# Pinning the recurrence's products in TensorE's queue to the order of the program

## The chip, the cores and the metric

The kernel runs on one core of a Trainium2 chip, in one launch. The metric is the device time of one execution, in microseconds (us); lower is better. Before the change the median of three runs is 3521.82 us.

## The reference, cut to what matters

The model is two transformer-like blocks of two layers each, over 512 latent tokens and, in the first block, 256 context tokens. The change touches one mixer of the first block alone, a gated linear recurrence (mLSTM) with 4 heads of 96 features, which runs forward and backward:

```python
dmat = jnp.where(tri, b[..., :, None] - b[..., None, :] + ib[..., None, :], -jnp.inf)
w_intra = jnp.exp(dmat - m_t[..., None])
s = jnp.einsum("bhtd,bhsd->bhts", qb, kb) * w_intra
num = jnp.einsum("bhts,bhsv->bhtv", s, vb) + ...
den = s.sum(axis=-1) + ...
h = num / jnp.maximum(jnp.abs(den), jnp.exp(-m_t))[..., None]
```

The kernel computes it without the carried state, as a masked quadratic form: for each head and direction, scores of keys against queries, times an exponential of gates, times the values.

## The kernel before

Activations lie with features on the 128 partitions and tokens along the free dimension. Most of the time goes into dense products of three passes each (`mm3`, lines 144, 145 and 147), whose weights SyncE loads, and ScalarE (`whi`, L121) and GpSimd (`wlo`, L122) split in two halves.

The recurrence is `mlstm`. It runs three times: over the context in layer 0 (one block of 256 queries), and over the latents in layers 0 and 1 (two blocks Q = 0 and 1). Below, a *stage* (Q, p) is one block Q of 256 queries against one pair p of key blocks of 128; p = 2 is the context. A latent recurrence goes through (0,2), (0,0), (0,1), (1,2), (1,1), (1,0). Where p equals Q a stage is diagonal: it holds both directions with a triangular mask; p = 2 has both directions without a mask; (0,1) and (1,0) have one direction.

- `scores` has four steps in a stage, one for each head. A step computes the scores of a head, two products (L953, tile `qM` by `kM` into a bank `pm`). For each direction it takes a bank `pt` and, for each of two key blocks kk, computes the gate rows into half of that bank (L960, `rows` by `sel`), adds the mask where the stage is diagonal (L964), reads the half with ScalarE's exponential into `D` (L966), and multiplies on VectorE into `W` (L968, L970). There are two `pt` banks and three `D` buffers, shared with other work.
- `values` follows for the stage before: in each of four steps (the ones column, then three columns of the values) every direction and key block gives four products, one for each head (L983). Each fills 32 of TensorE's 128 columns, at tile positions 0, 32, 64 and 96, and adds into the bank group `p`. Four such neighbours are called a quad here.
- `weave` alternates a step of scores and a step of values of the stage before. In the first stage there is no stage before, so its steps stand alone. After the last values of a block comes `mlstm_out` (den, L1014 to L1033), with three products at L1028 that need VectorE and ScalarE first, in another `pt` bank.
- Around the recurrence other generators are woven in: the Fourier mixer (L786 to L805) beside the first stage, and the first part of the output projection, groups of 15 products at L144, L145 and L147 (tiles `y` and `whi`, `wlo`), beside the stages from (1,2) on.

The program issues the products in this order, but the framework's scheduler does not keep it: on each engine it places instructions by its own estimate of when they are ready. The `pt` half of the second key block is written only after ScalarE has read the first half of that bank: each second L960 waits for the L966 before it.

A product with both operands in full fp32 (L953, L983, L1028) leaves two records in the trace, so "x28" of L983 is 14 products; L960 and L964 leave one.

Of the kernel before, what the change touches and what calls it, by code (L numbers as in the profile page):

```python
# [67 lines left out]
def weave(a, b, na, nb):  # L68

    credit = 0.0  # L70
    for _ in a:
        credit += nb / na
        while credit >= 1:
            credit -= 1
            if next(b, None) is None:
                credit = -1e9
        yield True
    for _ in b:
        yield True
# [10 lines left out]
class Kernel:  # L90
    def __init__(self, nc, tc, st, d, at):
# [10 lines left out]
        self.dram = pool("dram", 1, space=bass.MemoryType.DRAM)  # L102
        self.n_split = self.n_project = 0


    def col(self, name, i=0, n=1, rows=slice(0, 128)):
        o, m = self.at[name]
        assert i + n <= m
        return self.cols[rows, o + i:o + i + n]
# [812 lines left out]
    def mlstm(self, s, l, o, ctx, rows_cc, ys):  # L922
        nc, d, n = self.nc, self.d, s.n
        own = ctx is None
        nk = n if own else n + 256
        rows, cc, negm = rows_cc
        o["gm"] = self.times(f"gm{l}{s.name}", self.col(f"gm{l}", 0, 3), -0.5 / 96)
        VM, qk = o["VM"], o["qk"]
        q, k = [], []
        for h in range(4):  # L930
            t = self.new("hq", [96, n], "qM")
            nc.sync.dma_start(out=t, in_=qk[96 * h:96 * h + 96])
            q.append(t)
            t = self.new("hk", [96, nk], "kM")
            nc.sync.dma_start(out=t[:, 0:n], in_=qk[384 + 96 * h:480 + 96 * h])
            if not own:
                nc.sync.dma_start(out=t[:, n:], in_=ctx["kM"][384 + 96 * h:480 + 96 * h])
            k.append(t)
        nq = n // 256
        first = [] if own else [nq]  # L940
        acc, late = {}, iter(())

        def seen(Q, p, dr, kk):

            return slice(0, 256) if p != Q or kk == dr else slice(128 * kk, 128 * kk + 128)

        def scores(Q, p, dirs, W):
            cQ = slice(256 * Q, 256 * Q + 256)
            for h in range(4):
                sp = self.psum("pm", [128, 2, 256])  # L950
                for kk in range(2):
                    c = 256 * p + 128 * kk
                    nc.tensor.matmul(sp[:, kk], k[h][:, c:c + 128], q[h][:, cQ], start=True, stop=True)  # L953
                for dr in dirs:
                    rp = self.psum("pt", [128, 2, 256])
                    D = self.new("ta", [128, 2, 256], "D")
                    w = self.new("W", [128, 2, 256], "W")
                    for kk in range(2):
                        r = 32 * dr + 6 * h + 2 * p + kk
                        nc.tensor.matmul(rp[:, kk], self.sel2[:, r:r + 1].to_broadcast([128, 128]), rows[:, cQ],  # L960
                                         start=True, stop=p != Q)
                        if p == Q:

                            nc.tensor.matmul(rp[:, kk, 128 * kk:128 * kk + 128], self.identb, self.tri[:, dr], start=False, stop=True)  # L964
                        T = seen(Q, p, dr, kk)
                        nc.scalar.activation(out=D[:, kk, T], in_=rp[:, kk, T], func=AF.Exp, bias=cc[:, 2 * p + kk, r:r + 1])  # L966
                        if p == Q:
                            nc.vector.tensor_tensor(out=w[:, kk, T], in0=sp[:, kk, T], in1=D[:, kk, T], op=ALU.mult)  # L968
                    if p != Q:
                        nc.vector.tensor_tensor(out=w, in0=sp, in1=D, op=ALU.mult)  # L970
                    W[dr, h] = w
                yield True

        def values(Q, p, dirs, W, ends):
            for j in (3, 0, 1, 2):
                for dr in dirs:
                    if (Q, dr) not in acc:
                        acc[Q, dr] = self.psum("p2", [128, 4, 256])
                    for i, kk in enumerate((dr, 1 - dr)):
                        T = seen(Q, p, dr, kk)  # L980
                        for h in range(4):
                            lhs = VM[2 * p + kk][:, 96 * h + 32 * j:96 * h + 32 * j + 32] if j < 3 else self.ones[:, 0:32]
                            nc.tensor.matmul(acc[Q, dr][32 * h:32 * h + 32, j, T], lhs, W[dr, h][:, kk, T],  # L983
                                             start=p == ends[dr][0] and i == 0 and j in (3, 0),
                                             stop=p == ends[dr][1] and i == 1 and j in (1, 2), tile_position=(0, 32 * h))
                yield True

        for Q in range(nq):
            sets = [first + list(range(0, Q + 1)), first + list(range(Q, nq))]
            order = first + [Q] + [p for p in range(nq) if p != Q]  # L990
            lists = [[p for p in order if p in x] for x in sets]
            ends = [(x[0], x[-1]) for x in lists]
            for p in order:
                dirs = [dr for dr in range(2) if p in sets[dr]]
                W = {}
                yield from weave(scores(Q, p, dirs, W), late, 4, 4 if p != order[0] or not Q else 6)
                late = values(Q, p, dirs, W, ends)
                if p == order[-1]:
                    late = self.chain(late, self.mlstm_out(s, l, o, Q, acc, negm, ys))
        yield from late  # L1000
# [689 lines left out]
```

## Time and profile before

| | |
|---|---|
| median of 3 runs | 3521.82 us (3521.39 to 3522.93) |
| the profiled execution, its own time | 3521.57 us |
| span of its instructions | 3519.8 us |
| TensorE matmul busy | 3356.4 us, 95% of the span |
| VectorE, ScalarE, GpSimd busy | 49%, 45%, 32% |
| TensorE's mean granted clock | 0.977 of 2.4 GHz |
| the recurrence in the context | 190.8 to 220.5 us |
| the recurrence in the latents, layer 0 | 380.2 to about 500 us |
| the recurrence in the latents, layer 1 | 1371.2 to about 1496 us |

TensorE's busy time contains the modelled tails of its pipelined products: a product counts as busy for longer than it keeps the next one from starting. So the start of one product to the start of the next is the better measure of what it costs, and a full share of busy time does not say that the engine does useful work at its peak.

### The profile page before, as it was taken

To read this page: it belongs to the slowest core of one execution; us is meant where nothing else is said; L and a number is where in the kernel's file an instruction comes from. 1 tells how busy PE (TensorE), PEld (TensorE's weight loads), DVE (VectorE), ACT (ScalarE), POOL (GpSimd) and SP (SyncE) were. 2 spreads that over 40 slices of the span, in tenths; PEclk is the share of its full clock that TensorE was granted. 3 is DMA by queue.
4 is the path that set the end of the run, shared out by engine and by line. 5 is a ranking of instruction groups with operands and counts; after the bars stand their busy time and mean duration, and the time that the engine had idled before them with its cause. 6 is when DMAs were issued, how large, how long until landed. Compare 5 with 4: busy or idle time off the path is not lost.

```text
span 3519.8 us, 47211 instructions
## 1 busy us (share of the span) xinstructions
PE 3356.4 (95%) x18518; PEld 2632.2 (75%) x18518; DVE 1728.1 (49%) x2728; ACT 1583.8 (45%) x2824; POOL 1139.9 (32%) x539
## 2 busy tenths in 40 slices
PE   6999998999998899989999999999999999999999
PEld 4666667888887666678878657887888757888887
DVE  5754358443336763374325865464314756453111
ACT  5545445242234554353333666543334656543333
POOL 1222024222235321144444212444444312343443
PEclk8999999999999999999999999999999999999999
DMA  7722124333334321045442101236422101222222
GB/s 266 265 89 63 43 67 142 132 117 123 114 108 155 108 75 57 21 134 196 164 144 99 67 31 53 88 106 213 164 96 90 66 31 59 76 94 90 96 96 96
DMA packets 146705, 377.87 MB, mean 107 GB/s; under 512 B 16737, under 2 KB 32690, under 8 KB 146354
## 3 DMA queue, kind: packets, MB, share of 16 engines
q1 hardware_dynamic: 146482, 374.85, 31.7%
q8 instruction: 146, 2.39, 0.3%
q14 instruction: 77, 0.63, 0.1%
HBM read 363.48 MB, written 9.86 MB: 106 GB/s over the span
## 4 chain that ended last, share of the span: by engine, by line
PE 56%; DVE 8%; ACT 2%; DMA 2%; issue 1%; POOL 0%; SPq 0%; DVEq 0%; ACTq 0%; POOLq 0%
PE pm L144 14%; PE pm L145 14%; PE pm L147 13%; DMA g<-in_w_mod 1%; DVE y L360 1%; PE p L983 1%; PE p L1182 1%; PE pt L1200 1%; PE p L1227 1%; PE pt L1208 1%; PE pm L151 1%; PE pt L1248 1%; DVE h L388 1%; PE pt L145 1%; PE pm L953 1%
## 5 line engine op out<-in xcount | busy, mean ns | idle before, releaser
L122 POOL TENSOR_TENSOR wlo<-raw,whi 128x1024 fp32r<-128x1024 f32 (+2 forms) x461 | 1089.2, 2364 | 2189.9 <-ACT whi L121 2071.7
L121 ACT CAST whi<-raw 128x1024 fp32r<-128x1024 f32 (+2 forms) x468 | 476.8, 1019 | 1079.7 <-PE pm L145 603.1
L144 PE MATMUL pm<-h,whi 128*128 128x512 f32 (+1 forms) x2312 | 851.9, 377 | 11.3 <-DVE kr L676 5.0
L145 PE MATMUL pm<-h,whi 128*128 128x512 f32 (+1 forms) x2312 | 842.1, 372 | 2.8 <-DVE h L388 2.7
L147 PE MATMUL pm<-h,wlo 128*128 128x512 f32 x1816 | 718.1, 395 | 2.3 <-POOL wlo L122 2.3
L144 PEld LDWEIGHTS pm<-h,whi 128*128 128x128 f32 x2312 | 440.5, 191 | 107.8 <-issue 20.8
L145 PEld LDWEIGHTS pm<-h,whi 128*128 128x128 f32 x2312 | 439.9, 190 | 78.9 <-issue 5.8
L144 PE MATMUL pm<-hid,whi 128*128 128x512 f32 (+1 forms) x1280 | 457.3, 367 | 2.8 <-DVE x L459 1.5
L145 PE MATMUL pm<-hid,whi 128*128 128x512 f32 (+1 forms) x1280 | 456.2, 365 | 3.7 <-DVE hid L527 3.7
L147 PEld LDWEIGHTS pm<-h,wlo 128*128 128x128 f32 x1816 | 344.3, 190 | 76.2 <-POOL wlo L122 4.0
L147 PE MATMUL pm<-hid,wlo 128*128 128x512 f32 x976 | 381.3, 391 | 3.1 <-POOL wlo L122 3.1
L527 DVE TENSOR_TENSOR hid<-relu,hid 128x512 fp32r<-128x512 f32 (+1 forms) x169 | 180.0, 1069 | 335.4 <-ACT hid L526 335.2
L273 DVE SCALAR_TENSOR_TENSOR p<-g,svec,p 128x512 f32<-128x512 f32 x280 | 211.0, 753 | 253.8 <-DMA g<-in_w_mod 250.8
L459 DVE SCALAR_TENSOR_TENSOR x<-pm,mod,x 128x512 f32<-128x512 f32 (+1 forms) x184 | 125.4, 684 | 385.1 <-PE pm L147 379.3
L144 PEld LDWEIGHTS pm<-hid,whi 128*128 128x128 f32 x1280 | 241.4, 189 | 45.7 <-issue 4.3
L145 PEld LDWEIGHTS pm<-hid,whi 128*128 128x128 f32 x1280 | 241.1, 188 | 42.8 <-DVE hid L527 5.0
L147 PEld LDWEIGHTS pm<-hid,wlo 128*128 128x128 f32 x976 | 183.9, 188 | 42.6 <-POOL wlo L122 4.4
L521 ACT ACTIVATE relu<-pm 128x512 f32<-128x512 f32 (+1 forms) x160 | 85.4, 534 | 131.6 <-PE pm L147 131.6
L966 ACT ACTIVATE D<-pt,cc 128x256 f32<-128x256 f32 (+1 forms) x176 | 75.0, 447 | 97.4 <-PE pt L960 59.5
L339 DVE TENSOR_TENSOR acc<-acc,sq 128x256 f32<-128x256 f32 (+1 forms) x96 | 87.9, 916 | 29.1 <-ACT sq L331 27.6
L523 ACT ACTIVATE relu<-relu 128x512 f32<-128x512 f32 (+1 forms) x169 | 96.4, 570 | 4.7
L387 ACT ACTIVATE h<-y,mod 128x256 fp32r<-128x256 f32 (+1 forms) x136 | 67.2, 528 | 69.0 <-DVE y L360 68.2
(418 smaller groups left out, 4843.6 us busy)
## 6 DMA issues: line engine op xcount, KB each, us to landing
g<-in_w_mod SPq DMA_DIRECT2D x352, 256.0 KB, 3.4
raw<-in_w_in SPq DMA_DIRECT2D x142, 512.0 KB, 3.5
raw<-in_w_down SPq DMA_DIRECT2D x136, 512.0 KB, 3.5
raw<-in_w_up SPq DMA_DIRECT2D x128, 512.0 KB, 3.5
raw<-in_w_out SPq DMA_DIRECT2D x24, 512.0 KB, 3.4
g<-in_w_mod SPq DMA_DIRECT2D x16, 512.0 KB, 7.7
raw<-in_w_out SPq DMA_DIRECT2D x16, 384.0 KB, 3.3
raw<-in_w_br SPq DMA_DIRECT2D x16, 384.0 KB, 3.0
```

Source lines behind the costliest of these rows:

```text
L121: nc.scalar.copy(out=hi, in_=src)
L122: (eng or nc.vector).tensor_tensor(out=lo, in0=src, in1=hi.bitcast(F32), op=ALU.subtract)
L144: nc.tensor.matmul(out, hi[:, k], xh, start=i == 0, stop=False)
L145: nc.tensor.matmul(out, hi[:, k], xl, start=False, stop=False)
L147: nc.tensor.matmul(out, lo[:, k], xh, start=False, stop=i == n - 1)
L273: nc.vector.scalar_tensor_tensor(out=a, in0=g, scalar=sk, in1=a, op0=ALU.mult, op1=ALU.add)
L339: nc.vector.tensor_tensor(out=acc, in0=acc, in1=sq, op=ALU.add)
L459: nc.vector.scalar_tensor_tensor(out=x, in0=ps, scalar=ga[:, m:m + 1], in1=x, op0=ALU.mult, op1=ALU.add)
L521: nc.scalar.activation(out=r, in_=ps, func=AF.Relu)
L523: nc.scalar.activation(out=q, in_=r, func=AF.Square)
L527: nc.vector.tensor_tensor(out=lo, in0=q, in1=hi.bitcast(F32), op=ALU.subtract)
L966: nc.scalar.activation(out=D[:, kk, T], in_=rp[:, kk, T], func=AF.Exp, bias=cc[:, 2 * p + kk, r:r + 1])
```

## The change

A method `mm` issues a product and hands it to `keep_in_program_order`: the scheduler then keeps all products that were marked so in the order in which the program issues them, among themselves. All four products of `scores` and `values` go through it. Other instructions, TensorE's included (L1028, the Fourier mixer, the output projection), are placed by the scheduler as before, also between marked ones. No product is added or removed, and no operand, buffer or shape changes. On GpSimd and in SyncE's queue the order stays what it was; on VectorE and ScalarE a few dozen instructions trade places. All of it lies in the three recurrences. In the changed kernel all marked products have line 108, and other lines are numbered 4 higher.

```diff
+    def mm(self, *args, **k):
+        self.tc.keep_in_program_order(self.nc.tensor.matmul(*args, **k))
...
-                    nc.tensor.matmul(sp[:, kk], k[h][:, c:c + 128], q[h][:, cQ], start=True, stop=True)
+                    self.mm(sp[:, kk], k[h][:, c:c + 128], q[h][:, cQ], start=True, stop=True)
...
-                        nc.tensor.matmul(rp[:, kk], self.sel2[:, r:r + 1].to_broadcast([128, 128]), rows[:, cQ],
+                        self.mm(rp[:, kk], self.sel2[:, r:r + 1].to_broadcast([128, 128]), rows[:, cQ],
                                          start=True, stop=p != Q)
                         if p == Q:
-                            nc.tensor.matmul(rp[:, kk, 128 * kk:128 * kk + 128], self.identb, self.tri[:, dr], start=False, stop=True)
+                            self.mm(rp[:, kk, 128 * kk:128 * kk + 128], self.identb, self.tri[:, dr], start=False, stop=True)
...
-                            nc.tensor.matmul(acc[Q, dr][32 * h:32 * h + 32, j, T], lhs, W[dr, h][:, kk, T],
+                            self.mm(acc[Q, dr][32 * h:32 * h + 32, j, T], lhs, W[dr, h][:, kk, T],
```

TensorE, layer 0, stage (0,0), third head, from its first gate product on. `pt_3722` is the bank of the forward direction and `pt_3733` that of the backward one; `Activation_49` is ScalarE's semaphore. Before:

```order
L960 MATMUL pt_3722<-rows_2586,sel2_354 128x256 [waits Activation_49]
L964 LDWEIGHTS identb_338
L964 MATMUL pt_3722<-tri_340,identb_338 128x128
L960 MATMUL pt_3733<-rows_2586,sel2_354 128x256 [waits Activation_49]
L964 LDWEIGHTS identb_338
L964 MATMUL pt_3733<-tri_340,identb_338 128x128
L983 MATMUL p2_3657<-W_3545,VM_2896 32x256
L960 MATMUL pt_3722<-rows_2586,sel2_354 128x256 [waits Activation_49]
L964 LDWEIGHTS identb_338
L964 MATMUL pt_3722<-tri_340,identb_338 128x128
L983 MATMUL p2_3657<-W_3564,VM_2896 32x256
L960 MATMUL pt_3733<-rows_2586,sel2_354 128x256 [waits Activation_49]
```

The same place now:

```order
L108 MATMUL pt_3722<-rows_2586,sel2_354 128x256 [waits PE_49]
L108 LDWEIGHTS identb_338
L108 MATMUL pt_3722<-tri_340,identb_338 128x128
L108 MATMUL pt_3722<-rows_2586,sel2_354 128x256 [waits Activation_49]
L108 LDWEIGHTS identb_338
L108 MATMUL pt_3722<-tri_340,identb_338 128x128
L108 MATMUL pt_3733<-rows_2586,sel2_354 128x256 [waits PE_49]
L108 LDWEIGHTS identb_338
L108 MATMUL pt_3733<-tri_340,identb_338 128x128
L108 MATMUL pt_3733<-rows_2586,sel2_354 128x256 [waits Activation_49]
L108 LDWEIGHTS identb_338
L108 MATMUL pt_3733<-tri_340,identb_338 128x128
```

The two halves of a bank now follow each other directly; the backward direction's first half and the two single value products that stood between them come later, and all sixteen value products (L983 before) of the step follow as one run.

ScalarE at the same place, the four exponentials of this head. Before:

```order
L966 ACTIVATE D_3723<-pt_3722,cc_2583 128x256 [waits DVE_49,PE_49]
L966 ACTIVATE D_3734<-pt_3733,cc_2583 128x128 [waits DVE_49,PE_49]
L966 ACTIVATE D_3723<-pt_3722,cc_2583 128x128 [waits PE_49]
L966 ACTIVATE D_3734<-pt_3733,cc_2583 128x256 [waits PE_49]
L966 ACTIVATE D_3764<-pt_3763,cc_2583 128x256 [waits DVE_49,PE_49]
```

The same place now:

```order
L970 ACTIVATE D_3723<-pt_3722,cc_2583 128x256 [waits DVE_49,PE_49]
L970 ACTIVATE D_3723<-pt_3722,cc_2583 128x128 [waits PE_49]
L970 ACTIVATE D_3734<-pt_3733,cc_2583 128x128 [waits DVE_49,PE_49]
L970 ACTIVATE D_3734<-pt_3733,cc_2583 128x256 [waits PE_49]
L970 ACTIVATE D_3764<-pt_3763,cc_2583 128x256 [waits DVE_49,PE_49]
```

The second and the third have changed places.

TensorE, layer 0, where stage (1,1) begins and the output of block 0 ends (L1028 before, L1032 now, into `pt_4062`). Before, from the end of the value products that stand ahead of it:

```order
L983 MATMUL p2_4151<-W_4040,ones_83 32x256
L983 MATMUL p2_4151<-W_3928,ones_83 32x256
L1028 MATMUL pt_4062<-H_4059,bd32_346 128x256 [waits Activation_49] x3
L960 MATMUL pt_4120<-rows_2586,sel2_354 128x256
L964 LDWEIGHTS identb_338
L964 MATMUL pt_4120<-tri_340,identb_338 128x128
L983 MATMUL p2_4151<-W_3978,ones_83 32x256
```

The same place now:

```order
L108 MATMUL pm_4117<-qM_3520,kM_3522 128x256 [waits DVE_49,PE_49]
L108 MATMUL pm_4117<-qM_3520,kM_3522 128x256
L1032 MATMUL pt_4062<-H_4059,bd32_346 128x256 [waits Activation_49] x3
L108 MATMUL pt_4120<-rows_2586,sel2_354 128x256
L108 LDWEIGHTS identb_338
L108 MATMUL pt_4120<-tri_340,identb_338 128x128
L108 MATMUL pt_4120<-rows_2586,sel2_354 128x256 [waits Activation_49]
```

Before, thirteen value products stood between the score products and L1028; now the three products of the output follow the score products directly.

## Rows read from the trace of the kernel before

**Rows 1.** Windows: start:end, length, busy time of each engine, clock, DMA share, GB/s.
```profile
380.19:394.29 14.10, 13.19 (x55) 7.88 (x55) 7.35 (x13) 8.31 (x21) 0.00 (x0) 1.00 0.14 43
386.91:388.60 1.69, 1.69 (x7) 0.97 (x7) 0.69 (x1) 0.41 (x2) 0.00 (x0) 1.00 0.00 0
394.29:413.28 18.99, 18.99 (x165) 10.64 (x164) 7.76 (x21) 7.68 (x20) 0.00 (x0) 1.00 0.01 2
426.32:446.82 20.50, 20.29 (x129) 13.09 (x127) 7.66 (x13) 9.86 (x23) 1.55 (x1) 1.00 0.07 17
429.92:433.45 3.53, 3.53 (x18) 2.92 (x16) 0.69 (x1) 0.01 (x1) 0.00 (x0) 1.00 0.00 0
446.82:471.83 25.01, 24.74 (x199) 14.55 (x197) 12.87 (x33) 10.94 (x28) 5.21 (x5) 1.00 0.09 27
1371.22:1390.40 19.18, 17.95 (x86) 11.73 (x84) 7.82 (x15) 10.62 (x26) 1.54 (x1) 1.00 0.05 18
```

**Rows 2.** Timeline of TensorE, stage (0,0), third head: start, duration, instructions.
```profile
402.85 1.13 PE L953 MATMUL pm<-qM,kM 96*128 96x256 f32 x4
403.63 0.47 PE L960 MATMUL pt<-rows,sel 128*128 128x256 f32 x1
...
404.35 0.62 PE L983 MATMUL p<-W,VM 128*32 128x256 f32 x2
404.89 0.38 PE L960 MATMUL pt<-rows,sel 128*128 128x256 f32 x1
...
405.83 0.39 PE L960 MATMUL pt<-rows,sel 128*128 128x256 f32 x1
...
406.22 1.92 PE L983 MATMUL p<-W,VM 128*32 128x256 f32 x28
408.07 0.48 PE L953 MATMUL pm<-qM,kM 96*128 96x256 f32 x1
```

**Rows 3.** Timeline of ScalarE, the same head.
```profile
404.21 0.73 ACT L966 ACTIVATE D<-pt,cc 128x256 f32<-128x256 f32 x2 [2.19 <-PE pt L964]
405.39 0.37 ACT L966 ACTIVATE D<-pt,cc 128x128 f32<-128x128 f32 x1 [0.45 <-PE pt L964]
406.33 0.47 ACT L966 ACTIVATE D<-pt,cc 128x256 f32<-128x256 f32 x1 [0.57 <-PE pt L964]
```

**Rows 4.** Timeline of TensorE and ScalarE, end of stage (0,2); idle time in brackets.
```profile
393.12 0.75 PE L960 MATMUL pt<-rows,sel 128*128 128x256 f32 x2 [0.44 <-ACT D L966]
...
394.07 0.39 PE L960 MATMUL pt<-rows,sel 128*128 128x256 f32 x1
...
392.60 1.42 ACT L966 ACTIVATE D<-pt,cc 128x256 f32<-128x256 f32 x3 [0.40 <-PE pt L960]
...
394.50 0.84 ACT L966 ACTIVATE D<-pt,cc 128x256 f32<-128x256 f32 x2
```

**Rows 5.** Groups of TensorE by line: single value products in (0,2), layer 0, then layer 1.
```profile
L983 PE MATMUL p<-W,ones 128*32 128x256 f32 x10 | 2.5, 391 | 0.1
...
L983 PE MATMUL p<-W,ones 128*32 128x256 f32 x12 | 3.7, 389 | 0.0
```

**Rows 6.** Timeline of TensorE, stage (0,1), first head.
```profile
413.28 1.13 PE L953 MATMUL pm<-qM,kM 96*128 96x256 f32 x4
...
415.23 0.39 PE L960 MATMUL pt<-rows,sel 128*128 128x256 f32 x1
415.54 1.07 PE L983 MATMUL p<-W,ones 128*32 128x128 f32 x22
416.54 0.48 PE L953 MATMUL pm<-qM,kM 96*128 96x256 f32 x1
```

**Rows 7.** Timeline of TensorE, start of stage (1,1).
```profile
446.82 1.03 PE L953 MATMUL pm<-qM,kM 96*128 96x256 f32 x4
...
449.97 1.56 PE L1028 MATMUL pt<-H,bd 128*128 128x256 f32 x6 [0.27 <-ACT H L1027]
451.18 0.47 PE L960 MATMUL pt<-rows,sel 128*128 128x256 f32 x1
```

**Rows 8.** Timeline of TensorE, context, in a stretch at the lower clock.
```profile
205.42 2.08 PE L953 MATMUL pm<-qM,kM 96*128 96x256 f32 x4
```

## The prediction

> **What bounds the kernel now.** I read the windows by stage first [rows 1], then TensorE's timeline of one step [rows 2], then ScalarE's beside it [rows 3]. In the stages of the latent recurrence TensorE is busy nearly throughout: 18.99 of 18.99 us in (0,0), 20.29 of 20.50 in (1,2), 24.74 of 25.01 in (1,1), all at full clock [rows 1]. So the recurrence ends when TensorE ends, and a microsecond that its queue loses there is lost at the end. But the busy share hides that the two halves of a `pt` bank are bound to a round trip through ScalarE. In the third head of (0,0) the first gate product starts at 403.63 [rows 2], ScalarE begins to read it at 404.21 and the read takes 0.37 (128 wide) to 0.47 (256 wide) [rows 3]; only then can the second half be written. In between TensorE does the other direction's gate product and a single value product [rows 2]. Where nothing was there to do, at the end of (0,2), the wait shows: 0.44 us idle, ended by L966 [rows 4]. The order is what covers these waits, and the order is what changes.
>
> **The recurring wait.** Start to start, from rows:
> - Without a mask, gate product to ScalarE's start is 394.07 to 394.50, 0.43 [rows 4]; the mean of three reads there is 1.42 / 3 = 0.47, and TensorE restarts 0.05 after a read that began at 392.60 (392.60 + 0.47 to 393.12) [rows 4]. Round trip 0.95.
> - With a mask it is 403.63 to 404.21, 0.58 [rows 2, 3], so 0.58 + 0.47 + 0.05 = 1.10.
> - In the new order the other bank's first half stands behind that wait, so its read comes late too: issue of two gate products with masks (about 0.35 each, half of the 0.75 of two [rows 4]) and a read of 0.47 queued behind a read. That gives about 1.28 with a mask and 1.42 without (there both reads are 256 wide) from the restart to the fourth gate product.
>
> A gate product with what belongs to it takes about 0.35 of issue that would be spent anyway, so a wait exposes about 0.75 (first) and 0.55 to 0.7 (second): my estimate for the mean is 0.66. Following the new order there are some 30 waits with no other product in them in layer 0 and 26 in layer 1.
>
> What the trace shows of TensorE at such a wait: at the end of (0,2) it stood idle for 0.44 and then took the gate product, while the score products of the next stage came later [rows 4]. The Trainium skill, "TensorE: Matmul & The Clock Gate", section "Step-by-step: what each phase is for", speaks against the change: products stay in the order of the queue, and only weight loads are pulled ahead. By that rule the pinned queue lets nothing past, and the estimate by it is my sum below; if the engine could pass a waiting product, the waits would cost nothing and the sum would fall by about 56 x 0.66 = 37 us. The idle row agrees with the rule.
>
> **What a step costs now.** Scores 403.63 - 402.85 = 0.78 [rows 2]. Last gate product with mask to values 406.22 - 405.83 = 0.39 [rows 2]; without a mask 415.54 - 415.23 = 0.31 [rows 6]. A run of values, four quads, 408.07 - 406.22 = 1.85 [rows 2]; eight half-width and full products 416.54 - 415.54 = 1.00 [rows 6]; for sixteen of mixed widths I take 1.43, between the two. So:
> - diagonal: 0.78 + 1.10 + 1.28 + 0.39 + 1.85 = 5.40, against 408.07 - 402.85 = 5.22 in the dearest step of before [rows 2];
> - two directions, no mask, with the eight values of a one-direction stage: 0.78 + 0.95 + 1.42 + 0.31 + 1.00 = 4.46; without values about 3.4;
> - one direction: 0.78 + 0.95 + 0.31 + 1.43 = 3.47, against 416.54 - 413.28 = 3.26 [rows 6].
>
> **The stages, layer 0.**
> - (0,2): four steps x 3.4 = 13.6. Ten records of the Fourier mixer follow; six take 1.69 [rows 1], so ten take 2.8, of which about 0.6 lies in waits. 15.8 against 14.10 [rows 1]: **+1.7**. The five value products that filled this stage [rows 5] move to (0,0).
> - (0,0): 4 x 5.40 = 21.6 against 18.99: **+2.6**.
> - (0,1): 4 x 3.47 = 13.9 against 426.32 - 413.28 = 13.04 [rows 1]: **+0.9**.
> - (1,2): 4 x 4.46 = 17.8, and two groups of the output projection at 3.53 each [rows 1], of which 14 products in 30 stand in the waits: 17.8 + 7.1 - 3.3 = 21.6 against 20.50: **+1.1**.
> - (1,1): the three products at L1028 need ScalarE. Before, thirteen value products stood ahead of them and they started at 449.97 after 0.27 of idle [rows 7]. Now they follow the scores, which began at 446.82: the stall is 449.97 - 446.82 - 0.78 = 2.4. Then 451.18 - 449.97 = 1.2 for themselves [rows 7], 0.7 for a bank that ScalarE reads late (an estimate: one round trip less the issue), and a group of the projection, 3.53 less 1.4 inside waits: 21.6 + 2.4 + 1.2 + 0.7 + 2.1 = 28.0 against 25.01 [rows 1]: **+3.0**.
> - (1,0): one direction, values already in runs: 0.
>
> Sum 9.3 us.
>
> **Layer 1.** The order from (0,0) on is the same: 2.6 + 0.9 + 1.1 + 3.0 = 7.6. But (0,2) differs: six single value products leave it (twelve records, 3.7 us busy [rows 5], or 6 x 0.54 by 404.89 - 404.35 [rows 2] = 3.2), while Fourier products fill six of its eight waits. Two bare waits of 0.9 come: 19.18 [rows 1] - 3.2 + 1.8 = 17.8, **-1.4**. Its 19.18 - 17.95 = 1.23 of idle [rows 1] I leave as it is. Sum 6.2 us.
>
> **Context.** At the lower clock the scores take 2.08 where they take 1.13 at the full one [rows 2, 8]; ScalarE's round trip doesn't grow with that, so waits are a smaller part, and joined quads gain more. Bounds: by the (0,2) of layer 1 a loss of -1.4 times two, by that of layer 0 +1.7 times two. I take 0, with 3 to either side.
>
> **Other engines.** VectorE and ScalarE are busy 7.76 and 7.68 of 18.99 in (0,0) [rows 1], and their swaps follow TensorE's; I cost them at nothing, since TensorE's queue hides them. If that cover went, the join in (1,1) is where it would show, where ScalarE has 10.94 of 25.01 [rows 1] and for which the 0.7 stands. GpSimd and SyncE's queue keep their order: nothing. One stall of 2.4 at each join may lower the clock for a while; at half clock 3.4 us of products lose 1.7, which I add once.
>
> 9.3 + 6.2 + 0 + 1.7 = 17.2. On the profiled execution's own time, 3521.57 (the median is 0.25 higher, so the two agree), that makes **3539 us**. Its own range, with the waits' mean at 0.50 to 0.80 (56 x 0.15 = 8 to either side): 3531 to 3547.
>
> **Rivals.**
> - **A, the other side: only one wait in each step is exposed.** ScalarE may have read the second bank's first half by the time that the fourth gate product comes up; the place is the second wait of each two-direction step, and the first costs only the 0.44 that TensorE's one bare wait showed [rows 4]. Then 28 x 0.44 = 12 us of waits stand in place of 37, and the joined quads win: 3539 - 25 = 3514; 3508 to 3524. The case decides from a mean wait of 0.66 - 17.2 / 56 = 0.35 downward. For it: that row. Against it: that wait was partly covered by two gate products ahead of it, and each read must still follow 0.43 to 0.58 after its product [rows 2 to 4]. Chance 0.15, of which 0.07 is faster and 0.08 within the bound.
> - **B, the clock.** TensorE now rests for half a microsecond every microsecond or two where no values or Fourier products stand between: (0,2) and the join. If its granted clock falls to the 1.2 GHz level there, a step's 1.1 us of scores and 1.9 us of values double, as in the context [rows 8]: about 8 us for one recurrence in the latents, 16 for both: 3555, with 3547 to 3561. For it: rests in (0,2) rise to about a third of the stage. Against it: 0.91 us of rest in 14.10 left the clock at 1.00 [rows 1]. Chance 0.18. The Trainium skill, "TensorE: Matmul & The Clock Gate", section "A second HAM failure mode: psum-queue depth-cycling", describes this mechanism: short rests between groups that wait for their banks make the clock swing. No row of before shows it at rests of this size.
> - **C, absorbed behind the recurrence.** After the last stage TensorE may have other waits that end no later than before, so that half or more of the loss goes into them: 3527 to 3531. Against it: the output projection that follows needs the recurrence's last result. Chance 0.10, half of it within the bound.
> - **D, no effect.** The scheduler could have kept the order already. Against it: the order of the changed program, in which all sixteen values stand in one run. 3522, chance 0.02.
>
> **How the numbers follow.** Forecast 0.55, A 0.15, B 0.18, C 0.10, D 0.02. A measurement of this kernel can tell about 0.2%, 7 us, from no change: under 3514.8 is faster, over 3528.9 slower. Faster: A's 0.07. Within: A's 0.08 + C's 0.05 + D's 0.02 = 0.15. Slower: 0.55 + 0.18 + 0.05 = 0.78. The range takes in the forecast with its bounds, C, and B up to its middle; left out are most of A, D, and B's upper part, about 0.2: 3524 to 3555.
>
> **What would show it.** Right: stage lengths near 15.8, 21.6, 13.9, 21.6 and 28.0 in layer 0; bare idle of TensorE before gate products, ended by ScalarE's exponential, twice a step; value products in runs of 1.85; a wait of about 2.4 ahead of the three products at the join. If the steps without a mask come out under 3.0, the second wait is hidden, and A holds. A granted clock under 1.00 in the latent stages speaks for B. An end of the recurrence that is later by some 9 and 6 us, and a following stretch that is shorter, speaks for C. I would be wrong altogether if single value products cost the stages more than the 0.54 that I read, since all steps of before contain them and none of the new ones does.

## The result, and the profile after

The changed kernel takes 3557.09 us, the median of four runs (3550.43 to 3560.62), against 3521.61 of the kernel before: 1.0102 times as long, with a 95% interval of 1.0089 to 1.0114. It is slower by about 36 us. The forecast said 3539, so the direction was right and the loss twice as large; the time lies near the middle of rival B (3547 to 3561) and outside the range (3524 to 3555).

The profiled execution took 3559.13 us, with a span of 3557.3 and a mean granted clock of 0.972, against 3519.8 and 0.977 before. The whole loss of 37.5 us lies in the two latent recurrences. These are the windows of the changed kernel, from the first score product to the last value product, by stages as in [rows 1] (start:end, length, busy time of each engine, clock, DMA share, GB/s):

```profile
380.51:397.69 17.18, 12.77 (x43) 8.68 (x43) 9.39 (x16) 9.70 (x23) 0.00 (x0) 0.79 0.12 36
397.69:422.88 25.19, 21.07 (x178) 12.59 (x177) 6.33 (x17) 6.88 (x17) 0.00 (x0) 0.80 0.01 1
422.88:437.14 14.26, 12.00 (x156) 7.79 (x152) 2.77 (x4) 3.79 (x8) 0.00 (x0) 1.00 0.00 1
437.14:459.96 22.82, 20.07 (x131) 13.02 (x127) 6.87 (x11) 9.50 (x22) 1.54 (x1) 0.93 0.05 15
459.96:492.33 32.37, 25.19 (x199) 15.15 (x198) 12.82 (x34) 11.49 (x29) 5.26 (x5) 0.89 0.07 21
...
380.51:519.39 138.88, 117.03 (x955) 75.04 (x954) 46.96 (x96) 49.89 (x117) 9.91 (x8) 0.90 0.07 20
1392.94:1414.22 21.28, 16.45 (x73) 11.92 (x72) 9.60 (x17) 12.15 (x28) 1.55 (x1) 0.92 0.04 15
1414.22:1437.92 23.70, 19.58 (x177) 11.77 (x176) 7.78 (x20) 7.59 (x19) 0.00 (x0) 0.86 0.01 2
...
1452.18:1476.71 24.53, 21.78 (x131) 13.84 (x127) 6.85 (x11) 9.48 (x22) 1.54 (x1) 0.86 0.05 14
1476.71:1507.47 30.76, 23.59 (x198) 14.86 (x197) 12.83 (x34) 11.48 (x29) 5.29 (x5) 0.94 0.07 23
1392.94:1534.53 141.59, 119.33 (x984) 78.01 (x983) 44.67 (x91) 50.48 (x115) 11.48 (x9) 0.93 0.05 16
```

The same two recurrences before, whole:

```profile
380.19:499.04 118.85, 117.46 (x954) 72.75 (x954) 46.95 (x96) 49.09 (x117) 9.87 (x8) 1.00 0.08 23
1371.22:1495.02 123.80, 122.09 (x985) 76.61 (x983) 44.52 (x91) 49.57 (x115) 11.42 (x9) 1.00 0.06 18
```

They grew by 20.0 and 17.8 us. Two things are to be seen. TensorE's rest, the length less its busy time, was 1.4 and 1.7 us and is now 21.9 and 22.3. And the clock, 1.00 over both recurrences before, is 0.79 to 0.94 in (0,2), (0,0), (1,2) and (1,1) of either layer. Busy time stayed level (117.46 to 117.03, 122.09 to 119.33) because the runs of value products shortened it and the lower clock lengthened it.

The clock of a stage is a mean of two levels, 1.00 and 0.50 of 2.4 GHz. Ahead of its longest low stretch in layer 0 TensorE rested 0.56 and 0.81 us in one step of (0,2). The stretch runs from the end of (0,2) into (0,0); behind it the clock is 1.00 for the rest of (0,0), which has the same waits, and for all of (0,1):

```profile
393.95:407.60 13.65, 11.35 (x54) 6.71 (x53) 5.13 (x10) 4.68 (x11) 0.00 (x0) 0.50 0.04 11
407.60:437.14 29.54, 24.18 (x282) 15.22 (x281) 6.97 (x16) 8.52 (x20) 0.00 (x0) 1.00 0.00 1
```

In layer 1 it is alike: 0.50 from 1414.54, 0.3 us behind the end of (0,2), to 1421.36, and 1.00 from there into the second step of (1,2). The other low stretches lie inside (0,2), (1,2) and (1,1). So what (0,0) lost to the clock it lost in its first steps, behind the rests of (0,2).

The order does what was expected of it. TensorE's timeline of the third head of (0,0), the place of [rows 2]:

```profile
412.27 1.13 PE L108 MATMUL pm<-qM,kM 96*128 96x256 f32 x4
413.05 0.47 PE L108 MATMUL pt<-rows,sel 128*128 128x256 f32 x1
...
414.15 0.38 PE L108 MATMUL pt<-rows,sel 128*128 128x256 f32 x1 [0.56 <-ACT D L970]
...
414.42 0.36 PE L108 MATMUL pt<-rows,sel 128*128 128x256 f32 x1
...
415.32 0.38 PE L108 MATMUL pt<-rows,sel 128*128 128x256 f32 x1 [0.47 <-ACT D L970]
...
415.71 1.93 PE L108 MATMUL p<-W,VM 128*32 128x256 f32 x32
417.57 0.70 PE L108 MATMUL pm<-qM,kM 96*128 96x256 f32 x2
```

Each second half of a bank stands behind a rest that ScalarE's exponential ends, twice a step, and all sixteen value products (32 records) follow in one run. The step takes 417.57 - 412.27 = 5.30 us where 5.40 was worked out. The first head of the same stage is the same order at the lower clock:

```profile
397.69 1.91 PE L108 MATMUL pm<-qM,kM 96*128 96x256 f32 x4
...
400.51 0.58 PE L108 MATMUL pt<-rows,sel 128*128 128x256 f32 x1 [0.56 <-ACT D L970]
...
402.79 3.64 PE L108 MATMUL p<-W,ones 128*32 128x256 f32 x32
406.36 1.73 PE L108 MATMUL pm<-qM,kM 96*128 96x256 f32 x4
```

The rest is as long, but the value run takes 3.64 instead of 1.93, and the step 406.36 - 397.69 = 8.67. This is what the forecast lacked.

### The profile page after: what moved, and what is told of

Its sections match the earlier page's. It is cut to its first block, busy times and chain, and to the rows that moved or that the text cites. A ratio compares the mean times of both kernels' runs of the same rounds, so it can differ in the third digit from the quotient of the medians.

```text
span 3557.3 us, 47203 instructions
## 1 busy us (share of the span) xinstructions
PE 3348.2 (94%) x18518; PEld 2634.5 (74%) x18518; DVE 1728.7 (49%) x2728; ACT 1586.7 (45%) x2824; POOL 1141.2 (32%) x539
## 4 chain that ended last, share of the span: by engine, by line
PE 55%; DVE 6%; ACT 2%; issue 1%; POOL 0%; DMA 0%; ACTq 0%; POOLq 0%; DVEq 0%
PE pm L148 14%; PE pm L149 14%; PE pm L151 13%; PE p L108 1%; PE p L1186 1%; PE pt L1204 1%; PE p L1231 1%; DVE y L364 1%; PE pt L1212 1%; PE pt L149 1%; PE pt L148 1%; PE pm L108 1%; PE pt L1252 1%; PE pm L155 1%; PE pt L151 1%
## 5 line engine op out<-in xcount | busy, mean ns | idle before, releaser
L108 PE MATMUL pt<-rows,sel 128*128 128x256 f32 x176 | 69.5, 422 | 36.3 <-ACT D L970 36.3
```

The source lines that it names most:

```text
L108: self.tc.keep_in_program_order(self.nc.tensor.matmul(*args, **k))
```

## The experiments

The theory after the result: the waits without cover, less what whole runs of value products give back, cost some 15 to 20 us, about as forecast, and TensorE's rests in the waits bring its clock down, which costs as much again. Rivals: the clock falls because of the long runs of narrow value products; or pinning as such costs. All are timed against the kernel before on the same chip; ratios have their 95% interval. The medians of that kernel lie between 3517 and 3522 us, so two runs are compared below by how far each lies from its own runs of before.

### One part of the pinning alone

e1 pins the value products alone:

```diff
-                    self.mm(sp[:, kk], k[h][:, c:c + 128], q[h][:, cQ], start=True, stop=True)
+                    nc.tensor.matmul(sp[:, kk], k[h][:, c:c + 128], q[h][:, cQ], start=True, stop=True)
...
-                        self.mm(rp[:, kk], self.sel2[:, r:r + 1].to_broadcast([128, 128]), rows[:, cQ],
+                        nc.tensor.matmul(rp[:, kk], self.sel2[:, r:r + 1].to_broadcast([128, 128]), rows[:, cQ],
...
-                            self.mm(rp[:, kk, 128 * kk:128 * kk + 128], self.identb, self.tri[:, dr], start=False, stop=True)
+                            nc.tensor.matmul(rp[:, kk, 128 * kk:128 * kk + 128], self.identb, self.tri[:, dr], start=False, stop=True)
```

> Only the value products are pinned; score, gate and mask products are placed by the scheduler as before. The value products therefore stand in whole runs as in the changed kernel, but the waits between the two halves of a gate bank have other gate and score products in them. Theory (waits without cover cost some 19 us and the clock that falls because of them some 18 us): granted clock 1.00 in the stages of the latents and 3512 to 3525 us. Rival (the runs of value products, which fill 32 columns each, bring the clock down): a clock of 0.8 to 0.9 in (0,0) of the latents, as in the changed kernel, and over 3535 us.

Measured: 3499.88 us, 0.9945 (0.9927 to 0.9964), 21 us faster than before; the expected band was missed on the good side. The largest group of value products in layer 0, before and then e1 (busy, mean ns of one | idle):

```profile
L983 PE MATMUL p<-W,VM 128*32 128x256 f32 x383 | 34.6, 386 | 0.0
```

```profile
L108 PE MATMUL p<-W,VM 128*32 128x256 f32 x384 | 25.1, 383 | 0.0
```

One product takes as long as before, but more of them run at the same time: 34.6 us busy became 25.1. The Trainium skill, "TensorEngine Tiling (Array Packing)", section "Key Properties", states that tiles work independently and can run in parallel. The trace agrees: by [rows 2] one value product alone took 0.54 us from start to start, and four in a run 0.46. How much of the gain is this, and how much that TensorE changes less often from one kind of product to another, no run separates. In e1 the scheduler covers the gate waits with the other direction's gates and the next head's scores, and the clock in (0,0) is 1.00:

```profile
384.26:397.65 13.39, 13.27 (x139) 8.29 (x139) 6.57 (x17) 6.35 (x17) 0.00 (x0) 1.00 0.00 1
```

Only in (1,1), where the stall ahead of the join is left (2.1 us), is the clock 0.93, in both layers. So long value runs do not bring the clock down, and pinning as such does not cost.

e2 is the other part: scores, gates and masks pinned, values free.

```diff
-                            self.mm(acc[Q, dr][32 * h:32 * h + 32, j, T], lhs, W[dr, h][:, kk, T],
+                            nc.tensor.matmul(acc[Q, dr][32 * h:32 * h + 32, j, T], lhs, W[dr, h][:, kk, T],
```

> Score, gate and mask products are pinned, value products are placed by the scheduler, which puts some of them into the waits. Theory: where value products stand in the waits they are covered; the first stage of a block has few of them, so (0,2) loses some 2 us and its clock falls a little; 3528 to 3542 us. Rival (the runs of value products bring the clock down): clock 1.00 and no more than 3525 us, since the runs are broken up.

Measured: 3524.98 us, 1.0010 (1.0001 to 1.0019), below the band and barely clear of no change. The time is the rival's (no more than 3525), but e1 has ruled its reason out, and the clock is not 1.00 throughout. The scheduler puts the free value products into the waits: (0,0) has no rest and takes 19.64. (0,2), where few are ready, has 2.5 us of rest and in layer 0 a clock of 0.90 (in layer 1 it rests 2.4 and stays at 1.00):

```profile
394.06:413.70 19.64, 19.64 (x166) 10.96 (x165) 6.44 (x18) 6.67 (x17) 0.00 (x0) 1.00 0.01 2
376.81:394.06 17.25, 14.78 (x55) 8.66 (x55) 9.20 (x16) 9.70 (x23) 0.00 (x0) 0.90 0.13 38
```

One part gains 21 us, the other loses 4, both together lose 36. The loss belongs to the pair: either part leaves the scheduler something to put into the waits, and both together leave nothing.

### The waits taken away

e3 pins all four, but the program writes both halves of a bank before ScalarE reads either, so nothing makes the second half wait. e4 is the same edit with nothing pinned.

```diff
                     for kk in range(2):
                         r = 32 * dr + 6 * h + 2 * p + kk
...
+                    for kk in range(2):
+                        r = 32 * dr + 6 * h + 2 * p + kk
                         T = seen(Q, p, dr, kk)
                         nc.scalar.activation(out=D[:, kk, T], in_=rp[:, kk, T], func=AF.Exp, bias=cc[:, 2 * p + kk, r:r + 1])
```

> All four products pinned, but both halves of a gate bank are written before ScalarE reads either, so no gate product waits for a read of its own bank's first half. Runs of value products as in the changed kernel. Theory: no wait without cover is left but that of the join in (1,1); a diagonal step falls from 5.3 to 0.78 + 4 x 0.35 + 0.15 + 1.85 = 4.2 us, the clock stays 1.00 in the latents, and the whole is faster than the kernel before: 3500 to 3515 us. Rival (runs of value products, or pinning itself, bring the clock down): clock of 0.8 to 0.9 in (0,0) and over 3530 us.

> The kernel before, nothing pinned, with the one edit of the run before it here: both halves of a gate bank are written before ScalarE reads either. Theory: the scheduler then has few waits to fill and leaves most runs of value products whole by itself; 3500 to 3515 us, within 3 us of the pinned version. If pinning has a worth of its own once the waits are gone, the pinned version is over 3 us faster than this one.

Measured: e3 3496.19 us, 0.9931 (0.9909 to 0.9953); e4 3482.85 us, 0.9891 (0.9866 to 0.9916). Both are faster than expected, and the expectation that they lie within 3 us failed: pinning all four costs 13 us here too. The clock of e3 did not stay at 1.00 either: it is 0.87 in (1,1) of layer 0 and in (0,2) of layer 1, which rest 3.6 and 3.7 us. In (0,0) of layer 0, with whole value runs and no rest, it is 1.00. TensorE in one step of (0,0) of e3:

```profile
395.73 1.13 PE L108 MATMUL pm<-qM,kM 96*128 96x256 f32 x4
396.51 0.47 PE L108 MATMUL pt<-rows,sel 128*128 128x256 f32 x1
...
397.71 1.93 PE L108 MATMUL p<-W,VM 128*32 128x256 f32 x32
399.57 0.70 PE L108 MATMUL pm<-qM,kM 96*128 96x256 f32 x2
```

The step takes 399.57 - 395.73 = 3.84 us against 5.30, with the same pinned order of kinds and the same value run. The two waits were thus worth 1.46 a step at full clock. Of the 11.4 us that the latent recurrences of e3 lose against e4, 6.4 are lost in (1,1), where the pinned join stalls, and 3.9 in (0,2). Layer 0, e3 with 26.68 us at a clock of 0.87, then e4 with 22.37 at 1.00:

```profile
431.07:457.75 26.68, 23.06 (x199) 15.18 (x197) 12.86 (x33) 10.42 (x28) 5.20 (x5) 0.87 0.06 15
```

```profile
433.09:455.46 22.37, 21.90 (x199) 14.11 (x197) 12.78 (x33) 10.32 (x28) 5.23 (x5) 1.00 0.07 18
```

### The waits filled with work that nobody needs

To tell the wait's own price from the clock's, e7 leaves the order and adds 52 products: the second score product of each step is done once more, inside the first wait. e8 adds the same 52 outside of it, directly behind the two score products. The line that is added:

```diff
+                            self.mm(sp[:, 1], k[h][:, 256 * p + 128:256 * p + 256], q[h][:, cQ], start=True, stop=True)
```

> The changed kernel with 52 products more: in each step the second score product is done once more, in the first wait of the step, between the two gate products of a bank (its result is the same). About 0.45 us of the first wait's 0.56 to 0.7 us of rest is filled, the waits and the order stay. Theory (rests of TensorE bring the clock down): the clock of the latent stages rises from 0.79 to 0.93 to 0.95 to 1.00, and with more work done the kernel is 8 to 18 us faster than the changed one: 3540 to 3550 us. Rival (the clock falls for another reason): the clock stays, and the time is 3557 us plus what of the product does not fit, 0 to 10 us.

> Control for the run before it here: the same 52 products more, but directly behind the two score products, not in a wait. Both theories: each costs about 0.43 us on the path, 52 of them some 22 us, and the rests stay: 3570 to 3590 us, the clock of the stages as in the changed kernel, 0.8 to 0.95. If it is as fast as the one with the waits filled, the place of the work does not matter and the theory of rests falls.

Measured: e7 3541.65 us, 1.0068 (1.0046 to 1.0090); e8 3580.20 us, 1.0180 (1.0159 to 1.0201). Both times are as the theory of rests expected. The same work costs 38.6 us more outside the waits than in them. Each against its own runs of before, e7 lies 24.2 us above, e8 62.8 and the changed kernel 35.5: with more work done e7 is 11 us faster than the changed kernel, and e8 27 us slower. The clock of e7 is 1.00 in all stages but (1,1), where the stall at the join is left: 0.94 and 0.89, under the 0.95 expected. (0,0) in layer 0 and layer 1, first e7, then e8:

```profile
390.79:411.91 21.12, 18.93 (x185) 11.47 (x184) 6.54 (x18) 6.78 (x17) 0.00 (x0) 1.00 0.01 2
1399.52:1420.65 21.13, 18.94 (x186) 11.48 (x185) 8.19 (x21) 7.99 (x20) 0.00 (x0) 1.00 0.01 2
```

```profile
405.06:432.14 27.08, 22.94 (x185) 14.22 (x184) 6.33 (x17) 6.89 (x17) 0.00 (x0) 0.81 0.00 1
1426.02:1452.90 26.88, 22.75 (x185) 14.05 (x184) 7.04 (x19) 6.96 (x18) 0.00 (x0) 0.82 0.01 2
```

With the first wait filled, in (0,2) and in (0,0), the clock stays at 1.00 and (0,0) takes 21.1 us in both layers. So the pinned order without the clock costs 2.1 over the 18.99 of [rows 1], where 21.6 in all was forecast. That is a net price: the waits, less what the whole value runs give back.

### Where the clock falls

e6 leaves scores and gates free in the stages of the context's keys, (0,2) and (1,2), and pins the rest.

```diff
+            mm = self.mm if p != nq else nc.tensor.matmul
...
-                    self.mm(sp[:, kk], k[h][:, c:c + 128], q[h][:, cQ], start=True, stop=True)
+                    mm(sp[:, kk], k[h][:, c:c + 128], q[h][:, cQ], start=True, stop=True)
```

The gate and mask products change in the same way.

> The changed kernel, but in the stages against the context's keys, (0,2) and (1,2) of the latents, score and gate products are not pinned; value products are pinned everywhere, and in the other stages all is as in the changed kernel. Theory (TensorE's rests in (0,2) are what brings the clock down, and it comes back only in (0,0)): (0,2) falls by some 3 us, (0,0) has the same order as in the changed kernel and yet a clock of 0.95 or more and about 21 us instead of 25.2 and 23.7; about 3535 us. Rival (the waits or the value runs of (0,0) themselves bring the clock down): (0,0) stays at 0.80 to 0.86 and 24 to 25 us; about 3548 us.

Measured: 3530.62 us, 1.0036 (1.0024 to 1.0049). The time is near what the theory said; its place came out in one layer of two. (0,2) and (0,0) of layer 0, then of layer 1:

```profile
382.64:395.59 12.95, 10.91 (x43) 7.09 (x43) 7.36 (x13) 8.21 (x21) 0.00 (x0) 1.00 0.14 41
395.59:421.01 25.42, 21.29 (x177) 12.14 (x176) 8.22 (x21) 8.10 (x20) 0.00 (x0) 0.80 0.00 1
1382.57:1399.45 16.88, 14.94 (x73) 10.93 (x72) 7.77 (x14) 9.93 (x24) 1.55 (x1) 1.00 0.05 19
1399.45:1420.65 21.20, 17.01 (x179) 10.61 (x177) 9.13 (x22) 9.07 (x22) 0.00 (x0) 1.00 0.01 2
```

(0,2) rests 2.0 and 1.9 us and stays at 1.00 in both. Yet (0,0), in the same order in both layers, falls to 0.80 in layer 0 and not in layer 1. In layer 0 it fell twice:

```profile
396.93:403.75 6.82, 5.92 (x39) 3.12 (x40) 2.85 (x7) 2.11 (x5) 0.00 (x0) 0.50 0.01 2
417.41:420.82 3.41, 3.41 (x34) 1.43 (x33) 0.42 (x1) 0.47 (x1) 0.00 (x0) 0.50 0.02 5
```

The first fall stands behind a row of bare waits: TensorE rested 0.32, 0.20 and 0.56 us at the end of (0,2), which the free order still left there, and 0.56 in the first step of (0,0). In layer 1 (0,2) ends with Fourier and score products, and the profile shows no rest in its last 2.8 us. That much is with the theory. The second fall has only steps of (0,0) close ahead of it, so their rests can do it too; but the same steps in layer 1, and behind 407.60 in the changed kernel, did not. What decides stays open. The pair gives a price: the same order takes 25.42 at 0.80 and 21.20 at 1.00, 4.2 us apart, where 0.20 x 25.42 = 5.1 is the clock that was missing; the rest of it fell into waits.

### Shorter waits, and the join

e5 pins all four, and writes the first halves of both directions before the second halves, so that the other direction's gate product stands in each wait. e9 is the changed kernel with the three products of the join issued one step of scores later.

```diff
-                for dr in dirs:
...
-                    for kk in range(2):
+                for kk in range(2):
+                    for dr in dirs:
```

For e9 `mlstm_out` is cut behind the products that fill `H`, and its second part, `fin`, goes ahead of the next stage's values:

```diff
-                late = values(Q, p, dirs, W, ends)
+                late = self.chain(fin, values(Q, p, dirs, W, ends))
```

> The changed kernel, all four products pinned, with one other order of the program: in a step the first halves of both directions' banks are written, then the second halves. A second half still waits for ScalarE's read of its bank's first half, but the other direction's gate product stands in that wait. Theory: a diagonal step falls from 5.3 to about 4.6 us, so (0,0) is some 18.5 us; rests are shorter, so the clock of the latent stages is nearer to 1.00; 3505 to 3530 us. If the waits were not what pinning costs, this order has as many of them and the time stays over 3545 us.

> The changed kernel, all pinned, with the three products of the output of block 0 (L1032 in the changed kernel) and what follows them issued one step of scores later in the program, so that the first head's gate products of (1,1) stand ahead of them. Theory (the stall of 2.4 us ahead of these products is lost in each latent recurrence, and the rest brings the clock down in (1,1)): (1,1) falls from 32.4 and 30.8 to 27 to 29 us with a clock of 0.95 to 1.00, the whole to 3545 to 3552 us. If the stall only moves to other waits: (1,1) stays at 30 us and over, and the whole at 3553 to 3560 us.

Measured: e5 3527.25 us, 1.0024 (1.0012 to 1.0036); its (0,0) is 17.83 us at 1.00 in layer 1 and 20.20 at 0.84 in layer 0, around the 18.5 expected; the low stretch in layer 0 begins in (0,2) here too, at 388.82. One gate product of cover in a wait gives back 29 of the 36 us, with everything pinned. e9 3545.44 us, 1.0080 (1.0065 to 1.0095), 10 us better than the changed kernel, each against its own runs of before. Its (1,1), layer 0 and layer 1:

```profile
452.90:481.54 28.64, 24.99 (x213) 16.93 (x212) 11.85 (x31) 11.31 (x28) 5.47 (x5) 1.00 0.08 24
1463.47:1495.05 31.58, 28.13 (x213) 18.65 (x212) 11.93 (x31) 11.42 (x28) 5.46 (x5) 0.89 0.08 22
```

Layer 0 is as expected. Layer 1 is not: its clock fell again. The later join also moves a group of the output projection from (1,0) into (1,1), so only the sum of the two stages can be compared: 59.43 to 51.84 in layer 0, 57.82 to 54.80 in layer 1.

### A version that beats both

e10 is e4 with the value products pinned, and nothing else pinned, e11 is e4 with the later join, e12 is e10 with the later join.

> Both halves of a gate bank are written before ScalarE reads either, as in the two runs of before, and only the value products are pinned. Theory (pinning values joins what the scheduler still splits, pinning gates and scores is what costs 13 us of the fully pinned version): 3478 to 3486 us, as the unpinned one or up to 4 us faster. If pinned values are held up at the join (1,1) as in the first run, 3485 to 3492 us.

> The best version so far (both halves of a gate bank before the exponentials, nothing pinned) with the same later join. The scheduler already puts value products ahead of the join there, so a stall of 0.5 us or less is left: 3479 to 3484 us, no difference that can be measured.

> Both halves of a gate bank first, only the value products pinned, and the later join. Pinned values can't be put ahead of the join by the scheduler, and (1,1) was 24.3 and 24.5 us at a clock of 0.93 without the later join. Theory: (1,1) falls to 21.0 to 22.5 us at 1.00 and the whole by 4 to 7 us, to 3476 to 3480 us. If the stall stays, 3483 us.

Measured: e10 3483.55 us, 0.9900 (0.9882 to 0.9919); e11 3485.33, 0.9907 (0.9888 to 0.9926), 1 us above its band; e12 3479.74, 0.9896 (0.9878 to 0.9913). With e4's 0.9891 they can't be told apart. In the profiled executions the later join is worth something only where the values are pinned: (1,1) and (1,0) of layer 0 together take 49.35 us at 0.97 in e10 and 47.57 at 1.00 in e12, but 47.44 in e4 and 47.58 in e11. (1,1) of e12 alone took 26.00, not the 21.0 to 22.5 expected, as the group of the projection moved into it here too.

The order of the halves alone gives 38 us; pinning the values adds nothing to it that can be measured.

## Why the prediction was right or wrong

**What bounds it: right.** The loss of TensorE's queue in the stages, 37.8 us, is the loss of the span, 37.5. So rival C falls: of half or more that it wanted absorbed, the stretch behind the second recurrence took back 2.0 us, and the one between the two was 1.4 longer. D falls with the timeline above.

**The step: right.** 5.30 against 5.40 for the diagonal step; 14.26 against 13.9 for (0,1), which ran at 1.00 in both layers. Both waits of a step show, as rests of 0.56 and 0.47, so rival A falls, which had the second one hidden. Over a whole recurrence, layer 0 and layer 1, TensorE waited for ScalarE's exponential (us in total, times, longest):

```profile
PE pt L108 <- ACT D L970: 19.4, 32, 1.6
PE pt L108 <- ACT D L970: 16.4, 27, 1.6
```

That is 0.61 us of rest a wait, where some 30 and 26 waits of 0.66 were forecast. ScalarE's first read in the step above, beside [rows 3]:

```profile
413.62 0.47 ACT L970 ACTIVATE D<-pt,cc 128x256 f32<-128x256 f32 x1 [2.63 <-PE pt L108]
```

From the gate product at 413.05 to its read it is 0.57, and the fourth gate product starts at 415.32, 1.17 after the second at 414.15: 1.28 was taken.

**The sum of the stages: nearly right.** With the clock's share taken off by the pairs at unlike clocks, the stages come near the forecast. (1,2) has one order in both layers and took 22.82 at 0.93 and 24.53 at 0.86: 1.71 us for 3.43 - 1.60 = 1.83 of missing clock (length times one less the clock). (1,1) took 32.37 at 0.89 and 30.76 at 0.94: 1.61 for 1.71. By these, the pair of (0,0) in e6 (4.2 for 5.1) and that in e5 (20.20 at 0.84 and 17.83 at 1.00, 2.4 for 3.2) one us of missing clock costs 0.73 to 0.94; it is under 1 because a part of it falls into rests, which the clock does not lengthen. By these prices (1,2) at full clock is some 21.3 to 22.0 (21.6 forecast), (0,0) 21.1 to 21.2 by e7 and e6 (21.6), (1,1) 29.0 to 29.8 (28.0), and (0,2) of layer 0 13.8 to 14.5 (15.8), all estimates but (0,0). So the forecast is 1.3 to 2.0 too high in (0,2) and 1.0 to 1.8 too low in (1,1). The stall ahead of the three products is there, with 2.44 of rest (2.4 forecast); what was mis-sized is the wait of the bank behind it, where ScalarE comes from the join's own work:

```profile
459.96 1.03 PE L108 MATMUL pm<-qM,kM 96*128 96x256 f32 x4
463.43 1.56 PE L1032 MATMUL pt<-H,bd 128*128 128x256 f32 x6 [2.44 <-ACT H L1031]
464.64 0.47 PE L108 MATMUL pt<-rows,sel 128*128 128x256 f32 x1
...
466.82 0.38 PE L108 MATMUL pt<-rows,sel 128*128 128x256 f32 x1 [1.64 <-ACT D L970]
```

466.82 - 464.64 = 2.18 stands where a common wait is 1.10, so 1.1 and not 0.7. (0,2) of layer 1 was forecast to gain 1.4 and lost 2.1, of which the clock explains 1.2 to 1.6; the order that was to cover its waits with Fourier products has new ones, two of 0.71 ahead of score products among them:

```profile
1397.45 2.07 PE L790 MATMUL pm<-dftc,fold 128*128 128x128 f32 x8 [0.57 <-ACT dv L794]
...
1405.77 1.10 PE L108 MATMUL pm<-qM,kM 96*128 96x256 f32 x4 [0.71 <-PE pm L809]
```

**The clock: wrong, and nearly the whole error.** The step that failed is "One stall of 2.4 at each join may lower the clock for a while; at half clock 3.4 us of products lose 1.7, which I add once". The sum had a fall at the join alone, priced once, and no row stands behind its 3.4. The runs showed the clock at 0.50 for a part of (0,2), (0,0), (1,2) and (1,1) in both layers. The missing clock of the stages is 13.8 us in layer 0 (3.6 + 5.0 + 1.6 + 3.6) and 10.3 in layer 1 (1.7 + 3.3 + 3.4 + 1.8), and at 0.73 to 0.94 apiece that cost an estimated 18 to 23 us. The rest of the 37.8, 15 to 20, stands against the 15.5 that the forecast's stages sum to. This rest is a net price. TensorE's rest alone grew by 41 us, and the whole runs of value products hid a good part of that: e1, which has the runs and few of the waits, is 21 us faster than before, and e3, which has the pins and the runs without the waits between halves, 25, so 60 faster than the changed kernel. The runs of one kernel agree: the four of the changed kernel had clocks of 0.974, 0.973, 0.972 and 0.970 and took 3550, 3555, 3559 and 3561 us.

Rival B had the mechanism, nearly the price (16 us, 3555 in all), and most of the places: (0,2), whose low stretch runs on into (0,0), and the join in (1,1). The falls in (1,2), 5.0 of the 24 us of missing clock, it did not name. Its weight was put too low by one reading: that 0.91 us of rest in (0,2) left the clock at 1.00 [rows 1]. The new order rests 17.18 - 12.77 = 4.4 us there, several times as much, and the prediction itself had worked that out as a third of the stage. A row on small rests was taken as evidence on large ones. That the rests bring the clock down, e7 and e8 show with equal work, filled and not, and e1 and e3 show that the value runs do not. That rests of this size always do is not shown (e6). The Trainium skill, "TensorE: Matmul & The Clock Gate", section "A second HAM failure mode: psum-queue depth-cycling", describes this swing of the clock in a kernel whose products pause at each turn of the PSUM banks. The trace agrees, with 0.79 to 0.94 by stage where it was 1.00.

**The context: a little past its bound.** From its first score product to the next dense product, before and now:

```profile
190.83:220.50 29.67, 27.19 (x227) 19.34 (x225) 13.68 (x32) 11.65 (x31) 3.49 (x2) 0.83 0.17 54
```

```profile
197.01:223.04 26.03, 22.84 (x226) 17.66 (x224) 13.89 (x32) 11.41 (x31) 3.45 (x2) 0.93 0.19 62
```

It is 3.6 us shorter, where 0 with 3 to either side was forecast. The clock, lower than 1.00 before the change too, rose: 5.0 us of it were missing and now 1.8, which by the prices above is 2.4 to 3.0 of the 3.6. So the order itself gave about 1 us here, within the forecast's bound. The stretch began 6.2 us later than before and the latent recurrence of layer 0 0.3 us later; what the 3.6 did for the latents is not shown.

## What to carry to other kernels

Before you fix an order by hand, ask what each wait in it has as cover, and price the two parts of a pin apart and together: here one part gained 21 us, the other lost 4, and both lost 36. Where rests of TensorE grow from nothing to a fifth of a stage, price the clock as well as the rests; here it cost about half of the whole loss, by the estimate above. Look for it behind the stage with the barest waits: the low clock that began there was paid for in the next one. And look first at what makes the wait: to write both halves of a bank ahead of the first read took it away, and gave 38 us without pinning anything.

## What the runs showed of the hardware

More work in the right place made the kernel faster: 52 products that nobody needs, put into TensorE's rests, gave 11 us, and the same 52 beside them cost 27. The granted clock is at one of two levels, 1.00 or 0.50 of 2.4 GHz, and the means of 0.79 to 0.94 come from stretches at either. A fall lasts beyond the rests ahead of it: in the changed kernel the clock was still at 0.50 through a value run of 3.64 us in (0,0), with TensorE busy throughout. The fall is not a plain function of a stage's order: with the same order and about 2 us of rest in the stage ahead, one (0,0) of e6 ran at 0.80 and the other at 1.00, and the first had its rests at the end of that stage, the second earlier. In the changed kernel the later steps of (0,0), with two waits and a run of values each, and those of (0,1), with one wait, ran at 1.00. Six of the ten low stretches in the changed kernel's two latent recurrences begin within 0.8 us behind a step that rested 0.56 and 0.81 us, but one more such step, at 446.57, was followed by none. What decides between a fall and none was not settled.
